# Adaptive normalisation in three instructions per tile, and 56 weight parts moved to VectorE

## The chip, the cores and the metric

The kernel runs on one core of one Trainium2 chip. The metric is the device time of one execution in microseconds (us). The engines are TensorE (PE in the profile; its weight loads are PEld), VectorE (DVE), ScalarE (ACT), GpSimd (POOL) and SyncE (SP), each with a queue of its own that it works through in order.

## The reference

Two layers over 512 latent tokens `x` and 256 context tokens `cx`, 1024 channels, all in float32. What matters here is the modulated norm, which stands twice in each layer, and what is around it:

```python
def rms_norm(t, g):
    return t * rsqrt(mean(t * t, axis=-1) + EPS) * g
def modulate(h, shift, scale):
    return h * (1 + scale) + shift

for l in range(2):
    zx = modulate(rms_norm(x, g_norm1[l]), sh1x, sc1x) @ w_in[l]
    ...                                  # scan branch, gating branch, windowed attention, merged to m
    x = x + ga1x * (m @ w_out[l])
    x = x + ga2x * sq_relu_mlp(modulate(rms_norm(x, g_norm2[l]), sh2x, sc2x), w_ff1[l], w_ff2[l])
    # the same for cx with its own modulation, in layer 0 only (in layer 1 the context gives keys, values, states)
```

## The kernel before, in words

Activations lie transposed: `self.x` is eight tiles of 128 channels by 768 tokens (512 latent, 256 context). Every product of the dense layers is made of three matmuls in the type float32r. Each operand is a rounded high part and a low part (the operand less the high part), and the three are high x high, high x low, low x high. `weights` (line 562) loads a block of 128x1024 weights by a DMA of SP's queue into `wr`, ScalarE rounds it into `wh`, and the low part `wl` is one subtraction, on GpSimd while `self.aside` is set and on VectorE otherwise (line 570). There are three buffers each of `wr`, `wh` and `wl`. The activations that enter a product are split the same way by `split` (line 558), one instruction of ScalarE and one of VectorE.

`norm` (line 826) takes a stretch of tokens. `rms` (line 787) squares the eight tiles on ScalarE and adds them on VectorE, TensorE sums over channels, a chain of 12 tiny VectorE instructions makes the inverse root, and four (or two) more put it on diagonals, which TensorE spreads into PSUM as `p`. Then each of the eight tiles takes four steps: x times `p` on VectorE, scale and bias on ScalarE, rounding on ScalarE, the low part on VectorE.

`out_proj` (line 1350) makes the output projection of the channels `f` from 2 to 7 for one stream of tokens, then the norm of that stream, then the same for the other stream, so that one stream's products can run beside the other's norm. The streams are 512 and 256 tokens wide in layer 0 and 256 and 256 in layer 1. `ff` (line 1378) starts with `ff1(0)`, stream by stream. In layer 0 its tail makes the last `ff2` and the norm of the next layer by streams, then the keys and values (`kv_proj`, `kv_post`) of that layer. `self.aside` is set in the attention stages, in the second part of `out_proj` with `ff1(0)`, and in that tail.

The order of the work is not the program's. `Rec` records every operation, and `schedule` (from line 346 on) plays them through on five modelled engines and writes out an order for each. A candidate with the lower number goes first; weights are recorded as 190 places earlier than they stand, and readers of PSUM as 50 places earlier. `emit` issues that order, so all instructions have line 507. In the model a VectorE operation with two wide inputs in SBUF (`both`) takes longer while GpSimd computes, by the line that the diff changes. The inverse root's chain is a `bundle`, one operation that nothing is put into.

Of the kernel before, what the change touches and what calls it, by code (L numbers as in the profile page):

```python
# [18 lines left out]
F32 = mybir.dt.float32  # L19
# [3 lines left out]
AF = mybir.ActivationFunctionType  # L23
OP = mybir.AluOpType
# [22 lines left out]
PE, ACT, DVE, POOL, SP = range(5)  # L47
# [134 lines left out]
class Rec:  # L182
# [153 lines left out]
    def schedule(self):  # L336
# [31 lines left out]
        free = [0.0] * 5  # L368
# [7 lines left out]
        now = 0.0  # L376
# [3 lines left out]
        def push(t, kind, x):  # L380
            nonlocal seq
            seq += 1
            heapq.heappush(events, (t, seq, kind, x))
# [43 lines left out]
        while events:  # L427
            now = events[0][0]
            while events and events[0][0] <= now + 1e-6:
                _, _, kind, x = heapq.heappop(events)  # L430
                if kind == "rel":
                    used[x.tag] -= 1
                    places[x.tag].append(x)
                    live[x.tag][x.first:x.last + 1] -= 1
                    if x.early:
                        early[x.tag][x.early[0]:x.early[1]] -= 1
            for e in range(5):
                while free[e] <= now + 1e-6:
                    best = pick(e)
                    if best is None:  # L440
                        break
                    _, j, i = best
                    cand[e].pop(j)
                    op = ops[i]
                    for b in op.new:
                        if b.space == "dram":
                            continue
                        used[b.tag] += 1
                        b.early = None
                        b.prev = places[b.tag].pop(0)  # L450
                        if b.prev is None:
                            b.place = fresh[b.tag]
                            fresh[b.tag] += 1
                        else:
                            b.place = b.prev.place
                        if b.first > front:
                            b.early = (front, b.first)
                            early[b.tag][front:b.first] += 1
                    dur = op.dur
                    if op.both and free[POOL] > now and busy:  # L460
                        dur += min(0.7 * (free[POOL] - now), dur)
                    if e == POOL:
                        busy = not op.nbytes
                    if e == ACT and op.table and table not in op.table:
                        dur += 1283
                        table = op.table[0]
                    free[e] = now + dur
                    end = now + dur
                    if op.nbytes:
                        dma = max(dma, end) + op.nbytes / 360.0  # L470
                        end = dma + 1900
                    op.end = end
                    for b in op.psum:
                        b.acc[e] = end
                    order.append((now, i))
                    done[i] = True
                    push(free[e], "go", None)
                    for u in op.users:
                        q = ops[u]
                        r = end + (LAT if op.nbytes else LATS[e][q.eng])  # L480
                        q.ready = max(q.ready, r)
                        q.wait -= 1
                        if q.wait == 0:
                            bisect.insort(cand[q.eng], (q.prio, u))
                            push(q.ready, "go", None)
                    for b in op.bases:
                        b.left -= 1
                        b.end = max(getattr(b, "end", 0.0), end)
                        if b.left == 0 and b.space != "dram":
                            push(b.end + LAT, "rel", b)  # L490
                    while done[front]:
                        front += 1
# [35 lines left out]
class Net:  # L528
# [297 lines left out]
    def norm(self, l, n, hs, G, a, b):  # L826
        nc = self.nc
        (p, _, _), = self.rms([(a, b)])
        i = int(a >= SEQ)
        sh = 24 * n  # L830
        for k in range(KT):
            u = self.slot([128, b - a])
            nc.vector.tensor_mul(u, self.x[k][:, a:b], p)
            nc.scalar.activation(u, u, AF.Identity, scale=G[:, i, k:k + 1], bias=self.mod[l][:, i, sh + k:sh + k + 1])
            self.split(u, hs[k][0][:, a:b], hs[k][1][:, a:b])

    def fm(self, w, hs, W, kk=KT, off=0, stride=128):
        mm = self.nc.tensor.matmul
# [511 lines left out]
    def out_proj(self, l, W):  # L1350
        nc = self.nc
        ms = []
        for k in range(KT):
            h = self.slot([128, W], F32R)
            lo = self.slot([128, W], F32R)
            self.split(self.m[k][:, :W], h, lo)
            ms.append((h, lo))
        self.x = []
        for k in range(KT):
            xk = self.slot([128, W])  # L1360
            nc.sync.dma_start(xk, self.xsrc[k][:, :W])
            self.x.append(xk)
        for i in range(2 if W > SEQ else 1):
            nc.vector.tensor_scalar(self.mod[l][:, i, 16:24], self.mod[l][:, i, 16:24], 0.5, None, op0=OP.mult)
        for f in range(JOINT[0]):
            w = self.weights(l, B_O + f)
            self.residual(l, 16, self.fm(w, ms, W), f)
        hs = self.pairs(W)
        G = self.gain(l, 1, W)
        for z in self.streams(W):  # L1370
            self.aside = True
            for f in range(JOINT[0], KT):
                w = self.weights(l, B_O + f)
                self.residual(l, 16, self.fm(w, ms, [z]), f)
            self.norm(l, 1, hs, G, *z)
        return hs

    def ff(self, l, hs, W):
        nc = self.nc

        def ff1(c, parts):
            out = [(self.slot([128, W], F32R), self.slot([128, W], F32R)) for _ in range(4)]
            for z in parts:
                for j in range(4):
                    w = self.weights(l, B_F1 + 4 * c + j)
                    ps = self.fm(w, hs, z)
                    for p, a, b in ps:
                        r = self.slot([128, b - a])
                        nc.scalar.activation(r, p, AF.Relu)
                        nc.vector.tensor_mul(r, r, r)  # L1390
                        self.split(r, out[j][0][:, a:b], out[j][1][:, a:b])
            return out

        def ff2(c, z, parts):
            for j in range(4):
                w = self.weights(l, B_F2 + 4 * c + j)
                for i in range(2):
                    ps = self.fm(w, z, parts, kk=4, off=i * 128, stride=256)
                    self.residual(l, 40, ps, 2 * j + i)

        z = ff1(0, [[q] for q in self.streams(W)])
        self.aside = False
        for c in range(7):
            for _ in range(3):
                self.bg()
            z2 = ff1(c + 1, [self.parts(W)])
            ff2(c, z, self.parts(W))
            z = z2
        if l == DEPTH - 1:
            ff2(7, z, self.parts(W))  # L1410
            return
        self.aside = True
        self.mod_bias(l + 1, 0, 16)
        hs = self.pairs(TOK)
        G = self.gain(l + 1, 0, TOK)
        ps = [self.p1() for _ in range(6)]
        for q in self.streams(W):
            ff2(7, z, [q])
            self.norm(l + 1, 0, hs, G, *q)
        for toks in (range(4), range(4, 6)):  # L1420
            self.kv_proj(l + 1, hs, ps, toks)
            self.kv_post(l + 1, ps, (0, 1) if toks[0] == 0 else (2,))
        return hs, ps
# [151 lines left out]
```

## Time and profile before

| | |
|---|---|
| median of 3 runs | 2715.12 us (2712.99 to 2715.19) |
| profiled execution, its own time | 2712.24 us |
| its span, first to last instruction | 2710.5 us |
| TensorE busy | 2624.4 us (97%) |
| VectorE busy | 1868.3 us (69%) |
| ScalarE busy | 1239.8 us (46%) |
| GpSimd busy | 319.6 us (12%) |
[...]

The span leaves out 1.7 us of the profiled execution's own time. Busy shares are means over stages. A wait of an engine is shown in square brackets with the instruction that ended it.

### The profile page before, as it was taken

The page shows a single profiled execution, that of the slowest core. Times are in us where ns is not written, and L with a number is a line of the kernel's source. Part 1 is how long each engine was busy: PE and PEld are TensorE (multiplying, and loading weights), DVE is VectorE, ACT ScalarE, POOL GpSimd, SP SyncE. Part 2 cuts the span into 40 slices and gives each one's busy share as a digit, 9 for nine tenths or more (in the row PEclk, how much of TensorE's full clock was granted, in tenths as well). Part 3 has the DMA queues.
Part 4 walks back from the last instruction along what each step waited for, and adds up shares of the span by engine and source line. Part 5 has one row for each costly group of instructions (what it writes and reads, how often), then busy time and mean ns, then how long its engine had stood idle before and what let it go on. Part 6 is the DMA issues. An engine that isn't in the chain of part 4 may idle for free.

```text
span 2710.5 us, 38395 instructions
## 1 busy us (share of the span) xinstructions
PE 2624.4 (97%) x14916; PEld 2259.9 (83%) x14916; DVE 1868.3 (69%) x3528; ACT 1239.8 (46%) x2158; POOL 319.6 (12%) x229
## 2 busy tenths in 40 slices
PE   7999999989999999999999998999999999899999
PEld 4889988878898888888888877887888888888887
DVE  8887787996637758544444478999898666844444
ACT  4466668992122225222222254666996223532322
POOL 1111110111000034000000152120011001600000
PEclk9999999989999999999999989999999999999999
DMA  6112122456524423322222232122347555432322
GB/s 241 59 46 69 67 78 83 124 192 201 167 71 161 166 78 111 115 86 86 86 70 63 70 123 70 59 70 95 94 127 252 200 191 174 138 111 93 94 93 86
DMA packets 94391, 309.15 MB, mean 114 GB/s; under 512 B 11328, under 2 KB 11488, under 8 KB 94208
## 3 DMA queue, kind: packets, MB, share of 16 engines
q1 hardware_dynamic: 74592, 248.62, 28.6%
q0 software_dynamic: 10400, 37.09, 4.6%
q10 hardware_dynamic: 9216, 20.98, 2.0%
q8 instruction: 117, 1.92, 0.3%
q14 instruction: 66, 0.54, 0.1%
HBM read 270.99 MB, written 35.65 MB: 113 GB/s over the span
## 4 chain that ended last, share of the span: by engine, by line
PE 73%; DVE 12%; ACT 6%; DMA 4%; issue 4%; POOL 1%; POOLq 0%; SPq 0%; ACTq 0%; DVEq 0%
PE p L507 73%; DVE s L507 8%; ACT s L507 5%; DVE t L507 3%; DMA wr<-wmod 2%; DMA s<-wmod_k 1%; DVE junk L507 1%; POOL wl L507 1%; ACT wh L507 1%; DMA wr<-w 1%; ACT L507 1%; DVE wl L507 1%; DMA s<-x 0%; DMA gn<-qkg 0%; POOLq L1562 0%
## 5 line engine op out<-in xcount | busy, mean ns | idle before, releaser
L507 PE MATMUL p<-s,wh 128*128 128x512 f32 (+1 forms) x6816 | 1673.9, 353 | 6.3 <-DVE s L507 5.9
L507 PEld LDWEIGHTS p<-s,wh 128*128 128x128 f32 x6816 | 1194.7, 189 | 234.9 <-DVE s L507 7.8
L507 PE MATMUL p<-s,wl 128*128 128x512 f32 (+1 forms) x3408 | 1029.8, 352 | 0.3 <-POOL wl L507 0.3
L507 ACT ACTIVATE wh<-wr 128x1024 fp32r<-128x1024 f32 x340 | 360.4, 1061 | 929.6 <-PE p L507 648.1
L507 PEld LDWEIGHTS p<-s,wl 128*128 128x128 f32 x3408 | 572.2, 189 | 48.0 <-POOL wl L507 0.5
L507 DVE TENSOR_TENSOR wl<-wr,wh 128x1024 fp32r<-128x1024 f32 x240 | 294.7, 1228 | 288.3 <-ACT wh L507 285.8
L507 ACT ACTIVATE s<-p 64x128 f32<-64x128 f32 (+6 forms) x718 | 300.4, 452 | 209.8 <-PE p L507 196.1
L507 POOL TENSOR_TENSOR wl<-wr,wh 128x1024 fp32r<-128x1024 f32 x100 | 244.1, 2444 | 1202.7 <-ACT wh L507 1142.6
L507 DVE TENSOR_TENSOR s<-s,s 128x512 fp32r<-128x512 f32 (+5 forms) x409 | 333.8, 834 | 72.1 <-ACT s L507 68.6
L507 PE MATMUL p<-wh,s 128*128 128x256 f32 (+1 forms) x1472 | 303.7, 301 | 4.1 <-DVE s L507 3.5
L507 PE MATMUL p<-s,s 128*128 128x256 f32 (+3 forms) x1568 | 283.9, 322 | 22.5 <-ACT s L507 16.2
L507 ACT ACTIVATE s<-s 128x256 fp32r<-128x256 f32 (+6 forms) x349 | 203.5, 610 | 213.8 <-DVE s L507 201.2
L507 PEld LDWEIGHTS p<-s,s 128*128 128x128 f32 (+1 forms) x1568 | 222.1, 185 | 60.4 <-ACT s L507 21.1
L507 DVE SCALAR_TENSOR_TENSOR s<-p,mod,s 128x512 f32<-128x512 f32 (+1 forms) x222 | 138.1, 645 | 181.4 <-PE p L507 181.4
L507 PEld LDWEIGHTS p<-wh,s 128*128 128x128 f32 x1472 | 238.9, 191 | 16.8 <-DVE s L507 4.4
L507 DVE TENSOR_TENSOR s<-p,s 64x128 f32<-64x128 f32 (+4 forms) x444 | 201.9, 477 | 29.1 <-ACT s L507 23.1
L507 PE MATMUL p<-wl,s 128*128 128x256 f32 (+1 forms) x736 | 219.6, 298 | 0.4 <-DVE wl L507 0.4
L507 DVE SCALAR_TENSOR_TENSOR junk<-wr,condb 128x1024 bf16<-128x1024 f32 x128 | 156.4, 1222 | 73.1 <-DMA wr<-wmod 71.9
L507 PEld LDWEIGHTS p<-wl,s 128*128 128x128 f32 x736 | 140.2, 190 | 6.3 <-DVE wl L507 0.6
L507 ACT ACTIVATE s<-s,t,t 128x512 f32<-128x512 f32 (+1 forms) x128 | 109.8, 861 | 59.4 <-DVE t L507 59.2
L507 PE MATMUL p<-ident,s 128*128 128x128 f32 (+1 forms) x776 | 106.4, 279 | 23.8 <-DVE s L507 21.7
L507 DVE SCALAR_TENSOR_TENSOR s<-s,s 128x768 f32<-128x768 f32 x128 | 116.2, 950 | 12.5 <-ACT s L507 12.5
(87 smaller groups left out, 1322.7 us busy)
## 6 DMA issues: line engine op xcount, KB each, us to landing
wr<-w SPq DMA_DIRECT2D x340, 512.0 KB, 3.6
wr<-wmod SPq DMA_DIRECT2D x80, 512.0 KB, 4.0
gd<-s ACTq DMA_DIRECT2D x24, 384.0 KB, 2.9
s<-gd POOLq DMA_DIRECT2D x24, 384.0 KB, 5.8
s<-x SPq DMA_DIRECT2D x16, 384.0 KB, 6.4
gd<-s ACTq DMA_DIRECT2D x24, 256.0 KB, 2.1
s<-gd POOLq DMA_DIRECT2D x24, 256.0 KB, 5.6
s<-wmod_k SPq DMA_DIRECT2D x16, 256.0 KB, 6.4
```

The costliest lines, as they stand in the source:

```text
L507: ins = getattr(getattr(self.nc, name), method)(*[r(x) for x in a], **{q: r(x) for q, x in k.items()})
```

## The change

In `norm` the scale moves into VectorE's product with `p`, the shift and the rounding become one ScalarE instruction, and VectorE's second step adds the shift again before it takes off the high part. Two settings of `self.aside` go, so the weights' low parts of `out_proj` from `f` = 2 on, of `ff1(0)`, and of the tail of `ff` are taken on VectorE: 20 blocks in each layer and 16 in the tail, 56 of 100. The other 44, in the attention stages, stay on GpSimd. In `schedule` the modelled delay of a VectorE operation beside GpSimd's becomes all of the time that GpSimd still needs.

```diff
@@ schedule
                     if op.both and free[POOL] > now and busy:
-                        dur += min(0.7 * (free[POOL] - now), dur)
+                        dur += free[POOL] - now
@@ norm
             u = self.slot([128, b - a])
-            nc.vector.tensor_mul(u, self.x[k][:, a:b], p)
-            nc.scalar.activation(u, u, AF.Identity, scale=G[:, i, k:k + 1], bias=self.mod[l][:, i, sh + k:sh + k + 1])
-            self.split(u, hs[k][0][:, a:b], hs[k][1][:, a:b])
+            shift = self.mod[l][:, i, sh + k:sh + k + 1]
+            h, lo = (t[:, a:b] for t in hs[k])
+            nc.vector.scalar_tensor_tensor(u, self.x[k][:, a:b], G[:, i, k:k + 1], p, op0=OP.mult, op1=OP.mult)
+            nc.scalar.activation(h, u, AF.Identity, bias=shift)
+            nc.vector.scalar_tensor_tensor(lo, u, shift, h.bitcast(F32), op0=OP.add, op1=OP.subtract)
@@ out_proj
         for z in self.streams(W):
-            self.aside = True
             for f in range(JOINT[0], KT):
@@ ff, tail
-        self.aside = True
         self.mod_bias(l + 1, 0, 16)
```

## Rows read from the trace of the kernel before

**Rows 1.** Stages: us, busy PE, PEld, DVE, ACT, POOL, granted clock, DMA share, GB/s.

```profile
960.00:1015.00 55.00, 55.00 (x274) 46.09 (x273) 26.25 (x22) 14.90 (x20) 19.89 (x9) 1.00 0.26 78
1015.00:1042.00 27.00, 22.69 (x156) 20.58 (x155) 23.56 (x39) 17.53 (x27) 17.55 (x7) 0.94 0.37 120
...
1530.00:1600.00 70.00, 63.40 (x321) 54.19 (x320) 48.20 (x104) 30.04 (x45) 32.67 (x22) 0.90 0.34 111
1600.00:1640.00 40.00, 33.53 (x149) 27.59 (x148) 32.03 (x75) 19.80 (x38) 19.16 (x8) 0.91 0.37 120
1640.00:1860.00 220.00, 206.37 (x1346) 180.98 (x1344) 197.41 (x559) 138.72 (x318) 41.25 (x17) 0.98 0.19 62
...
2280.00:2370.00 90.00, 81.31 (x561) 76.20 (x560) 67.36 (x108) 46.77 (x85) 48.83 (x20) 0.94 0.40 126
```

**Rows 2.** Timeline of TensorE: start, us, engine, instruction, idle before it and releaser.

```profile
1041.34 0.50 PE L507 MATMUL p<-s,wh 128*128 128x512 f32 x1 [1.80 <-DVE s L507]
...
1575.09 1.87 PE L507 MATMUL p<-ones,s 128*128 128x1 f32 x8 [2.78 <-DVE s L507]
...
1593.20 1.22 PE L507 MATMUL p<-wh,s 128*128 128x512 f32 x2 [3.20 <-DVE s L507]
...
1636.37 0.66 PE L507 MATMUL p<-ident,s 128*128 128x128 f32 x2 [6.47 <-DVE s L507]
...
2345.02 1.01 PE L507 MATMUL p<-ones,s 128*128 128x1 f32 x4 [4.64 <-DVE s L507]
```

**Rows 3.** TensorE alone in stretches of 3 us: busy time, granted clock, DMA.

```profile
1578.00:1581.00 3.00, 3.00 (x16) 0.50 0.58 175
...
1596.00:1599.00 3.00, 3.00 (x9) 0.53 1.03 415
```

**Rows 4.** Timeline, GpSimd (first row) and VectorE, with the count of merged instructions.

```profile
1014.83 2.38 POOL L507 TENSOR_TENSOR wl<-wr,wh 128x1024 fp32r<-128x1024 f32 x1 [3.17 <-ACT wh L507]
...
1015.30 2.45 DVE L507 TENSOR_TENSOR s<-s,s 128x512 f32<-128x512 f32 x1 [0.91 <-ACT s L507]
...
1036.40 4.89 DVE L507 TENSOR_TENSOR s<-s,s 128x512 fp32r<-128x512 f32 x2
...
1548.83 2.03 DVE L507 TENSOR_TENSOR t<-t,t 128x16 f32<-128x16 f32 x1
...
1573.18 1.85 DVE L507 TENSOR_TENSOR s<-s,s 128x512 f32<-128x512 f32 x1 [0.30 <-ACT s L507]
...
1591.24 3.71 DVE L507 TENSOR_TENSOR s<-s,s 128x512 fp32r<-128x512 f32 x4
...
1621.12 1.78 DVE L507 TENSOR_SCALAR t<-t 128x16 f32<-128x16 f32 x4
...
1628.45 2.30 DVE L507 TENSOR_TENSOR t<-t 128x16 f32<-128x16 f32 x1
...
2318.70 1.92 DVE L507 TENSOR_TENSOR s<-s,s 128x256 f32<-128x256 f32 x1 [0.49 <-ACT s L507]
...
2329.99 0.76 DVE L507 TENSOR_TENSOR s<-s,s 128x256 fp32r<-128x256 f32 x2
...
2356.54 5.28 DVE L507 TENSOR_TENSOR s<-s,s 128x256 fp32r<-128x256 f32 x3 [0.20 <-ACT s L507]
```

**Rows 5.** All the instructions of `wl` on GpSimd: ns minimum/median/maximum, first and last start.

```profile
L507 POOL TENSOR_TENSOR wl<-wr,wh x100: 2339/2407/3179, 50.7 to 2366.8; 128x1024 fp32r<-128x1024 f32 x100
```

**Rows 6.** Groups by form, whole span: busy us, mean ns, idle before, releasers.

```profile
L507 DVE TENSOR_TENSOR wl<-wr,wh 128x1024 fp32r<-128x1024 f32 x240 | 294.7, 1228 | 288.3 <-ACT wh L507 285.8
...
L507 DVE SCALAR_TENSOR_TENSOR s<-p,mod,s 128x512 f32<-128x512 f32 x138 | 103.3, 749 | 176.6 <-PE p L507 176.6
...
L507 ACT ACTIVATE s<-s 128x512 fp32r<-128x512 f32 x124 | 76.8, 628 | 95.2 <-DVE s L507 92.2 <-DMA s<-ya 2.0 <-DMA gd<-s 0.5
...
L507 ACT ACTIVATE s<-s,mod,G 128x512 f32<-128x512 f32 x24 | 18.7, 806 | 12.5 <-DVE mod L507 10.1 <-DVE s L507 1.2 <-DVE G L507 1.2
...
L507 DVE TENSOR_TENSOR s<-s,p 128x512 f32<-128x512 f32 x16 | 9.7, 680 | 0.5 <-PE p L507 0.5
```

## The prediction

> **What bounds the kernel now.** I read the stages first, then TensorE's waits in them, then VectorE and GpSimd side by side at the places where TensorE waits. TensorE is busy 97% of the span, so only its gaps, and the time that it runs at a lower clock behind them, can be won. The change touches three regions, and all three have gaps: 960 to 1075 us (second part of the output projection and `ff1(0)`, layer 0), 1530 to 1640 (tail of layer 0, keys and values of layer 1) and 2280 to 2370 (as the first, layer 1). TensorE idles 4.3 us of 1015 to 1042, 6.6 and 6.5 us in the two halves of the second region and 8.7 us in the third [rows 1]. The big waits are all for VectorE: 1.80, 2.78, 3.20, 6.47 and 4.64 us [rows 2].
>
> Behind such a wait the granted clock falls: to 0.50 in 1578 to 1581 and 0.53 in 1596 to 1599, after the waits that ended at 1575.09 and 1593.20 [rows 2, 3]. [...] I read about 6.5 us at that level behind the wait of 2.78 us and 5.5 us behind that of 3.20 us, estimates from such stretches; half of each is lost, 3.2 and 2.8 us. A gap thus costs up to twice what it shows.
>
> Why VectorE is late is seen beside GpSimd. GpSimd's low part runs from 1014.83 to 1017.21. VectorE's addition of 512 columns starts at 1015.30 and ends at 1017.75, 2.45 us, where a product of that size takes 0.68 [rows 4, 6]. It stands still until GpSimd is done. The same happens to instructions of 16 columns, 2.03 us at 1548.83 and 2.30 at 1628.45 [rows 4]. GpSimd is hardly held in return: median 2407 ns, minimum 2339 [rows 5].
>
> **The change part by part.** *Low parts on VectorE.* Removed are 56 GpSimd instructions and every stretch that they cause; added are 56 VectorE instructions of 1.228 us, 68.8 us in all [rows 6]. Where TensorE sets the pace this is hidden: in 960 to 1015 VectorE is busy 26 of 55 us and TensorE all of it [rows 1]. Where VectorE sets the pace, stretch goes out and work comes in, and I set one against the other by place. The stretch of a row is its time less that of unstretched neighbours (0.76 us for two of 256 columns [rows 4], about 0.65 each for 512).
>
> *Norm.* Per 512-column tile ScalarE had 806 + 628 = 1434 ns and will have one instruction with one pointer operand in place of two and a copy. I take the middle, 717 ns; the bounds are 628 and 806 [rows 6]. So a tile's first pair comes some 0.7 us earlier. VectorE's two steps go from about 0.68 each towards 0.749, the three-operand form that reads PSUM and a pointer [rows 6]: +0.13 us a tile, with bounds 0 and +0.2 (the second step doubled), about +1 us for eight tiles of 512 and as much, taken alike, for eight of 256. [...]
>
> *Planner.* The old line granted a blocked operation at most its own duration again: a 16-column one could grow by 0.16 us and grew by 2. The new line costs what the rows show. It can only change orders, now mostly in the attention stages, where 44 of the GpSimd instructions stay. I take 0 there and bounds of 5 us either way, since in layer 1's attention VectorE is busy 197 of 220 us and TensorE idles 13.6 [rows 1].
>
> Now by place.
>
> A, layer 0's output projection. From 1013.6 to 1045.6 VectorE works almost without pause until the first stream's last pair is out, and TensorE waits for pairs. Five stretched rows, the first at 1015.30 and the last at 1036.40 [rows 4], hold 1.8 + 0.6 + 2.1 + 1.3 + 3.6 = 9.3 us. Seven low parts start there: 8.6 us in. The norm adds 1.0. That is -0.3; but VectorE idled 3.7 us there, waiting for ScalarE and TensorE, and the new instructions can fill some 2 of it, and the second stream's norm loses a stretch before a wait of 1.25. Gain 2.5 us, bounds 0 and 7 (all gaps and the slow clock gone).
>
> B1, the wait of 2.78 us at 1575.09. It ends a chain of VectorE and ScalarE that began at 1546. Five stretched rows, 1548.83 to 1573.18 [rows 4], hold 1.85 + 2.15 + 1.2 + 1.2 + 1.15 = 7.6 us. Six low parts come in, 7.4 us, of which 3.4 fit in VectorE's pauses while ScalarE squares. Net 3.6, more than the wait. With 3.2 us of slow clock the place holds 6. Gain 4, bounds 0 and 6.
>
> B2, the wait of 3.20 us at 1593.20 for the first low part. Products of the first eight tiles start at 1586.46; the first subtractions stand in one stretched row of four at 1591.24 [rows 4]. After the change the first tile needs 0.68 + 0.72 + 0.75 and some 0.4 of hand-over: 1589.0. TensorE had its other work until 1588.6. Wait and slow clock hold 6.0 us. Up to three weights' low parts, 3.7 us, may go ahead of that tile. Gain 4, bounds 1 and 6.
>
> B3, the wait of 6.47 us at 1636.37 for the keys. The root's chain held four stretched rows from 1621.12 to 1628.45, 1.1 + 2.15 + 2.15 + 2.1 = 7.5 us. Being a bundle it takes in no low part. But three blocks of the attention stay on GpSimd in 1625 to 1633, and can now meet the rotation that follows: three times about 1.8 us. Gain 4.5, bounds 1 (7.5 less 5.4, less ordering) and 8 (with the clock). [...]
>
> C, layer 1's output projection. From 2318.7 to 2364.5 VectorE sets the pace through both norms. Seven stretched rows, 2318.70 to 2356.54 [rows 4], hold 1.5 + 2.1 + 3.6 + 2.0 + 2.5 + 2.0 + 4.2 = 17.9 us. Ten low parts come in, 12.3 us, and the two norms add 1.9. Net 3.7, and 1.3 of VectorE's pauses filled. Gain 5, bounds 0 and 9.
>
> Sum: 2.5 + 4 + 4 + 4.5 + 5 = 20 us. The profiled execution's own time, 2712.24, would become 2692.2. It lies 2.9 us below the median of the runs, 2715.12, to which the same sum gives 2695.1. I predict 2695.
>
> **The rivals.** *Even exchange.* VectorE gets as much work as stretch goes, and the pauses aren't filled. A gives -0.3, B1 7.6 - 7.4, C 3.7 - 2 for pauses that new waits open; with the low bounds of B2 and B3 that is about 4 us: 2711. For it: in A stretch and work are 9.3 and 9.6. Against it: B3's chain takes in nothing, and B2's tile is shorter whatever the order. Chance 0.18.
>
> *Slower: low parts put ahead of the norm.* Weights have 190 places of priority, so wherever `wh` is out a 1.228 us instruction stands before the norm's steps. In `ff1(0)` of layer 1 four blocks of a stream need 4 x (0.75 + 1.23) us for their squares, splits and low parts beside a norm of 8 x 0.82: 14.5 us of VectorE against about 11.3 of TensorE (four blocks of 24 matmuls at 0.118 us, estimates from the timeline). That opens 3.2 us, and a slow clock behind it 2 more. The like at A, with 4, and two such at B: 2715.1 + 5 + 6 + 5 less B3's 4.5 and what C gains, 5, about 2722. It decides where three or more of VectorE's low parts stand together before a first tile. Against it: TensorE consumes a block in 2.8 us or more, so there is room for only one at a time, and three buffers keep the lead short. Chance 0.10.
>
> *Attention reordered.* The new planner line moves the attention of layer 1, and 5 us are lost or won there. Lost, the time is 2700; won, 2690; both inside the range. Chance that this outweighs the three places: 0.06, half to each side of 0.
>
> The forecast, a gain of 8 to 32 us, keeps 0.66.
>
> **How the numbers follow.** A measurement of this kernel tells about 0.2%, 5.4 us, from no change. Faster by more: 0.66, a third of the even exchange (0.06) and half of the reordering (0.03), 0.75. Same: the rest of the even exchange (0.12) and 0.02: 0.14. Slower: 0.10 and 0.01, 0.11. The range reaches up into the even exchange, 2711. Below, all upper bounds together would give 36 us, 2679; that all come is unlikely, and I set 2681. Outside lie the slower rival and the ends, 0.2.
>
> **What would show it.** Right: 44 low parts on GpSimd and 296 on VectorE; no VectorE instruction of 16 or fewer columns above 1 us in the three regions; one ScalarE instruction a tile, near 0.72 us at 512 columns; waits of TensorE below 1.5 us at B1 and B2; B3 shorter; GpSimd idle in 960 to 1075. The granted clock of 1530 to 1640 should rise from 0.90 to above 0.95. Wrong: low parts of weights on VectorE as the releasers of TensorE's waits, waits in C as long as before with VectorE busy throughout, or new waits in the attention stages. The prediction falls if VectorE's pauses can't take the added work, since the exchange itself is near even.

## The result, and the profile after

The changed kernel takes 2685.91 us (median of four runs, 2684.32 to 2689.07) against 2715.14 before. The ratio is 0.9896, with a 95% interval of 0.9879 to 0.9913. That is 28 us faster by the ratio, where 20 were forecast; the time lies inside the range, near its lower part.

The head of the page after: span, then busy time of each engine.

```profile
span 2683.6 us, 38320 instructions
...
PE 2611.7 (97%) x14916; PEld 2250.1 (84%) x14916; DVE 1860.0 (69%) x3584; ACT 1217.8 (45%) x2108; POOL 182.6 (7%) x173
```

VectorE has 56 instructions more and is busy 8 us less. So 69 us of new work took the place of about as much standing still. By busy time alone the change is an even exchange, and yet the span is 27 us shorter.

The stages after (columns as in [rows 1]), cut where TensorE has done as much work as at the cuts before: a cut lies where it has started matmuls of as many columns, counted from the start, as in the kernel before at 1015, 1042, 1530, 1600, 1640, 1860, 2280 and 2370 us.

```profile
1005.90:1027.50 21.60, 20.78 (x155) 19.15 (x154) 20.70 (x42) 12.45 (x18) 0.00 (x0) 1.00 0.49 148
...
1513.50:1578.20 64.70, 59.09 (x321) 50.27 (x320) 51.26 (x110) 25.69 (x37) 4.34 (x8) 0.97 0.38 123
1578.20:1610.10 31.90, 31.85 (x147) 25.90 (x146) 27.62 (x69) 15.77 (x29) 5.40 (x3) 1.00 0.31 98
1610.10:1834.50 224.40, 208.22 (x1345) 182.31 (x1344) 204.36 (x573) 140.90 (x320) 42.16 (x18) 0.98 0.20 64
1834.50:2259.60 425.10, 417.15 (x2173) 350.51 (x2172) 337.49 (x507) 250.23 (x362) 31.00 (x52) 1.00 0.54 171
2259.60:2343.60 84.00, 78.89 (x561) 74.11 (x560) 62.72 (x130) 40.23 (x68) 0.00 (x0) 0.96 0.48 139
```

The stage from 1860 to 2280 us is not in [rows 1]; before, it was:

```profile
1860.00:2280.00 420.00, 415.30 (x2167) 349.82 (x2168) 335.68 (x504) 252.23 (x364) 30.14 (x52) 1.00 0.54 172
```

TensorE idles 0.8 us in place of 4.3 in the first row, 0.1 for 6.5 in the third and 5.1 for 8.7 in the last, and the granted clock is higher in these three and in the second (over the whole span 0.992 in place of 0.986). The second still idles 5.6 (6.6 before). Two stages became longer: layer 1's attention takes 224.4 us for 220 and idles 16.2 for 13.6, and what lies behind it takes 425.1 for 420.0 and idles 8.0 for 4.7.

TensorE's larger waits after, as in [rows 2]:

```profile
1024.64 0.50 PE L507 MATMUL p<-s,wh 128*128 128x512 f32 x1 [0.65 <-DVE s L507]
...
1572.57 1.22 PE L507 MATMUL p<-wh,s 128*128 128x512 f32 x2 [4.92 <-DVE s L507]
...
1627.00 0.63 PE L507 MATMUL p<-ident,s 128*128 128x128 f32 x4 [1.57 <-DVE s L507]
...
2332.14 0.58 PE L507 MATMUL p<-s,wh 128*128 128x256 f32 x1 [2.21 <-DVE s L507]
```

The waits of 2.78, 6.47 and 4.64 us are gone or small. That of 3.20 us, for the first low part in the tail of layer 0, has grown to 4.92.

The forms that the change made or moved, whole span:

```profile
L507 DVE TENSOR_TENSOR wl<-wr,wh 128x1024 fp32r<-128x1024 f32 x296 | 361.4, 1222 | 316.4 <-ACT wh L507 313.5
...
L507 POOL TENSOR_TENSOR wl<-wr,wh 128x1024 fp32r<-128x1024 f32 x44 | 106.8, 2433 | 534.6 <-ACT wh L507 534.3 <-POOL wl L507 0.4
...
L507 DVE SCALAR_TENSOR_TENSOR s<-s,mod,s 128x512 fp32r<-128x512 f32 x16 | 11.0, 744 | 0.0
L507 DVE SCALAR_TENSOR_TENSOR s<-s,G,p 128x512 f32<-128x512 f32 x16 | 10.9, 741 | 0.0
L507 ACT ACTIVATE s<-s,mod 128x512 fp32r<-128x512 f32 x16 | 10.6, 715 | 3.4 <-DVE s L507 3.4
```

ScalarE's step takes 715 ns where 717 was taken as the middle; VectorE's two take 741 (from PSUM) and 744 (from SBUF), where 749 was the estimate. The two differ by 3 ns.

Where the time came from is read best by stages of equal work, cut in every kernel's trace as above. S0 is layer 0's attention (60 to 400 us in the kernel before), A layer 0's output projection with the start of `ff1(0)` (1015 to 1100), B1, B2 and B3 are the places of the prediction in the tail of layer 0 (1530 to 1575, 1575 to 1600, 1600 to 1640), S1 is layer 1's attention (1640 to 1860), M what lies behind it (1860 to 2280), and C layer 1's output projection (2280 to 2370). The table gives, for one profiled execution of each kernel, the time of a stage against that of the kernel before, in us.

| kernel | S0 | A | B1 | B2 | B3 | S1 | M | C | span |
|---|---|---|---|---|---|---|---|---|---|
| the change | -7.3 | -7.8 | -2.9 | -2.3 | -8.1 | +4.0 | +5.3 | -5.9 | -26.9 |
| planner's line alone | -7.4 | -0.6 | -1.3 | -0.8 | -8.4 | +5.4 | +5.7 | +7.0 | -3.6 |
| norm alone | +0.1 | +0.8 | -1.4 | -3.6 | +4.1 | +1.2 | +4.5 | +1.9 | +4.1 |
| low parts on VectorE alone | +0.1 | -9.0 | -2.9 | -2.3 | -3.6 | +2.0 | +5.3 | -8.1 | -20.3 |
| planner and low parts | -7.3 | -9.0 | -2.9 | -2.2 | -8.1 | +4.5 | +7.2 | -8.0 | -27.1 |
| low parts twice | -7.4 | +2.0 | -3.0 | +4.7 | -8.1 | +9.0 | +6.5 | +10.1 | +9.6 |
| layer 0's attention on VectorE too | -11.4 | -7.7 | -2.9 | -2.2 | -8.1 | +4.6 | +7.2 | -5.3 | -28.0 |
| layer 1's attention on VectorE too | -7.4 | -7.8 | -2.9 | -1.9 | -7.7 | -7.7 | +8.1 | -6.4 | -37.5 |
| all on VectorE | -11.9 | -7.7 | -2.9 | -1.7 | -7.7 | -7.6 | +5.4 | -5.0 | -41.9 |
| pairs first | -7.3 | -8.7 | -3.0 | -8.1 | -7.8 | +9.0 | +8.7 | -8.6 | -30.5 |
| all on VectorE, pairs first | -12.0 | -8.6 | -3.0 | -8.0 | -7.8 | -2.3 | +5.5 | -8.4 | -44.7 |
| the same, norm in four steps | -12.1 | -9.2 | -3.0 | -4.4 | -8.4 | -3.0 | +7.8 | -8.4 | -41.4 |

The orders differ between kernels, so a stage is the same amount of TensorE's work and only nearly the same matmuls. The stretches left out are edited by no run (the first norm of layer 0 has code of its own and keeps its four steps). One of them, 1100 to 1530 us, agrees within 0.6 us in all kernels; the others, ahead of 60 and from 400 to 1015 us, differ by up to some 3 from kernel to kernel. A single difference below 3 us is therefore not read here.

### The profile page after: what moved, and what is told of

The parts are those of the page before. It is cut to its first block, busy times and chain, and to the rows that moved or that the text cites. A ratio compares the mean times of both kernels' runs of the same rounds, so it can differ in the third digit from the quotient of the medians.

```text
span 2683.6 us, 38320 instructions
## 1 busy us (share of the span) xinstructions
PE 2611.7 (97%) x14916; PEld 2250.1 (84%) x14916; DVE 1860.0 (69%) x3584; ACT 1217.8 (45%) x2108; POOL 182.6 (7%) x173
## 4 chain that ended last, share of the span: by engine, by line
PE 79%; DVE 10%; ACT 6%; issue 2%; DMA 2%; SPq 0%; POOL 0%; ACTq 0%; DVEq 0%; POOLq 0%
PE p L507 79%; DVE s L507 7%; ACT s L507 5%; DVE t L507 2%; DVE wl L507 1%; DMA s<-wmod 1%; ACT wh L507 1%; ACT L507 1%; DVE junk L507 1%; DMA wr<-wmod 0%; DMA wr<-w 0%; DMA s<-wmod_k 0%; DMA s<-gd 0%; SPq L507 0%; POOL s L507 0%
## 5 line engine op out<-in xcount | busy, mean ns | idle before, releaser
L507 DVE TENSOR_TENSOR wl<-wr,wh 128x1024 fp32r<-128x1024 f32 x296 | 361.4, 1222 | 316.4 <-ACT wh L507 313.5
L507 PE MATMUL p<-s,s 128*128 128x256 f32 (+3 forms) x1568 | 286.9, 324 | 17.9 <-ACT s L507 13.6
L507 DVE TENSOR_TENSOR s<-s,s 128x512 fp32r<-128x512 f32 (+5 forms) x361 | 260.3, 735 | 53.8 <-ACT s L507 51.2
L507 ACT ACTIVATE s<-s 128x512 fp32r<-128x512 f32 (+6 forms) x301 | 183.7, 631 | 189.0 <-DVE s L507 175.9
L507 PEld LDWEIGHTS p<-s,s 128*128 128x128 f32 (+1 forms) x1568 | 221.6, 185 | 50.0 <-ACT s L507 17.9
L507 POOL TENSOR_TENSOR wl<-wr,wh 128x1024 fp32r<-128x1024 f32 x44 | 106.8, 2433 | 534.6 <-ACT wh L507 534.3
L507 PE MATMUL p<-ident,s 128*128 128x128 f32 (+1 forms) x776 | 112.3, 280 | 18.4 <-DVE s L507 16.0
```

The source lines that it names most:

```text
L507: ins = getattr(getattr(self.nc, name), method)(*[r(x) for x in a], **{q: r(x) for q, x in k.items()})
```

## The experiments

**One part at a time.** Four kernels take the change apart. The planner's line alone:

```diff
-                        dur += min(0.7 * (free[POOL] - now), dur)
+                        dur += free[POOL] - now
```

> The planner's line alone; norm in four steps and all 100 low parts on GpSimd as before. Theory 1 (the places): the gain of the change in 960 to 1085, 1530 to 1640 and 2280 to 2370 us comes from taking GpSimd's low parts out. Then this run keeps only what was gained ahead of the first output projection (about 9 us there), gives some of it back in layer 1's attention, and ends at 2704 to 2713. Theory 2 (the planner): the orders were wrong because the model did not know the delay, and knowing it is most of the gain. Then TensorE's waits in the three regions shrink with GpSimd still at work in them, and the time is 2690 to 2698.

Measured: 2707.0 us, ratio 0.9974 (0.9964 to 0.9983), 7 us faster. Theory 1 holds. The gain, 7.4 us, lies in layer 0's attention, before any instruction that the rest of the change edits; as much is lost again in layer 1's output projection, where GpSimd is still at work. At B3 8.4 us are won, and the two stages behind it lose 11. TensorE's waits of this kernel in 2260 to 2375 us (total, times, longest):

```profile
PE p L507 <- DVE s L507: 9.5, 5, 4.3
```

One sign of theory 2 came true all the same. TensorE's wait for the keys, 6.47 us before, is 0.76 here, although VectorE still stands still beside GpSimd in the root's chain ahead of it (2.33 us for 16 columns, 0.18 in the changed kernel):

```profile
1609.89 2.33 DVE L507 TENSOR_TENSOR t<-t 128x16 f32<-128x16 f32 x1
...
1623.37 0.44 PE L507 MATMUL p<-ident,s 128*128 128x128 f32 x2 [0.76 <-DVE s L507]
```

With the new line the planner puts matmuls of 256 columns ahead of this one that stood behind it before.

The norm alone, with its three instructions as in the diff of the change:

```diff
-            nc.vector.tensor_mul(u, self.x[k][:, a:b], p)
-            nc.scalar.activation(u, u, AF.Identity, scale=..., bias=...)
-            self.split(u, ...)
+            nc.vector.scalar_tensor_tensor(u, self.x[k][:, a:b], G[:, i, k:k + 1], p, op0=OP.mult, op1=OP.mult)
+            nc.scalar.activation(h, u, AF.Identity, bias=shift)
+            nc.vector.scalar_tensor_tensor(lo, u, shift, h.bitcast(F32), op0=OP.add, op1=OP.subtract)
```

> The norm in three steps alone, planner and low parts as before. Theory 1: a first pair comes some 0.7 us earlier per norm and VectorE's steps are 0.13 us longer; 2710 to 2716. Theory 3 (ScalarE): the chain of the norm hangs on ScalarE's two steps, and the shorter chain is worth 8 us or more: below 2707.

Measured: 2715.15 us, ratio 1.0008 (0.9999 to 1.0018). The norm in three steps is worth nothing by itself, as theory 1 had it. Theory 3 falls.

The low parts on VectorE alone:

```diff
         for z in self.streams(W):
-            self.aside = True
...
-        self.aside = True
         self.mod_bias(l + 1, 0, 16)
```

> The 56 low parts on VectorE alone, norm in four steps and the old planner line. Theory 1: 2695 to 2703, no stretched VectorE row left in the three regions, and nothing changed ahead of 960 us. Theory 2: VectorE takes as much work as stretch goes, and the time is within 6 us of before.

Measured: 2690.91 us, ratio 0.9916 (0.9901 to 0.9931), 23 us faster, which is more than theory 1 had allowed. This is the change's core, and most of it lies in the two output projections (A and C in the table). Theory 2 falls for the low parts. At the keys a wait of 3.78 us is left, so there the low parts take away less than half of the 6.47 us:

```profile
1619.65 0.56 PE L507 MATMUL p<-ident,s 128*128 128x128 f32 x2 [3.78 <-DVE s L507]
```

The planner's line and the low parts, with the norm in four steps:

> Planner's line and low parts on VectorE, norm in four steps. Theory 1: the norm's part is 3 us or less, so 2686 to 2691. Theory 3: at least 8 us slower than the whole change, 2694 or more.

Measured: 2685.89 us, ratio 0.9899 (0.9884 to 0.9914): the whole change, within the intervals, so the norm adds nothing here either. 23, 7 and -2 us by the parts add up to the 28 of the whole.

**The same work twice.** If new work on VectorE costs little because it falls into pauses, more of it should cost little too. `twice` is set where the change took `aside` away.

```diff
         (self.nc.gpsimd if self.aside else self.nc.vector).tensor_sub(lo, raw, hi.bitcast(F32))
+        if self.twice:
+            self.nc.vector.tensor_sub(lo, raw, hi.bitcast(F32))
```

> The changed kernel, but each of the 56 low parts on VectorE is written twice, so 68 us more of VectorE's work in the three regions, known to the planner. Theory 1a (what counts is where the work lies): a low part on VectorE falls into its pauses or behind work that TensorE does not wait for, and costs little; the second ones cost 10 us or less, 2686 to 2696. Theory 1b (the prediction's bookkeeping): a low part takes its 1.23 us from VectorE's chain wherever VectorE sets the pace, 8.6 us in A, 4 in B and 12.3 in C; the second ones cost 20 to 30 us, 2706 to 2716.

Measured: 2724.47 us, ratio 1.0047 (1.0032 to 1.0062), some 40 us more than the changed kernel for 68 us of work. Theory 1a falls, and 1b was still too cheap. Against the change the doubled parts cost 10 us in A, 7 at B2, 16 in C and 5 in layer 1's attention, which this run does not edit; at B1 and B3 they cost nothing. Its waits of TensorE for VectorE, in 960 to 1100 and in 2240 to 2400 us:

```profile
PE p L507 <- DVE s L507: 8.1, 2, 7.8
...
PE p L507 <- DVE s L507: 14.9, 5, 5.0
```

So in A, at B2 and in C VectorE's work lies on the path. That the first set of low parts nevertheless came with a gain of 23 us means that the stretch which it replaced, with the GpSimd work that made it, had cost more than the low parts do. Each of the two prices by itself was not measured.

**The attention stages.** The same exchange was made where the change leaves it out, first in layer 0 alone (the diff below) and in layer 1 alone (with `l == 0` in its place):

```diff
-            self.aside = True
+            self.aside = l > 0
             self.attention(l, hs, W, ps)
```

> The changed kernel with the 24 low parts of layer 0's attention on VectorE too. About 23 us of stretch goes from 62 to 400 us and 29 us of work comes. Theory 1a: the work can be put aside and the stretch could not, so TensorE's waits there (5 us for VectorE) shrink: 2680 to 2685. Theory 1b: an exchange that costs 6 us of VectorE, of which TensorE's pace hides most: 2685 to 2690.

Measured: 2684.71 us, ratio 0.9900 (0.9885 to 0.9915): nothing beside the change's 0.9896, and no decision between the two theories. In its trace the stage itself is 4.1 us shorter than the change's (S0 in the table), and the rest of the kernel loses about as much.

> The changed kernel with the 20 low parts of layer 1's attention on VectorE too. About 32 us of stretch goes from 1600 to 1860 us and 24 us of work comes, in a stage where VectorE is busy nine tenths of the time. Theory 1a: 2674 to 2682. Theory 1b: the net of 8 us is seen at most in part: 2680 to 2684. A rival (VectorE becomes the bound): its queue is full there, and the time is 2686 or more.

Measured: 2675.78 us, ratio 0.9868 (0.9851 to 0.9884), 8 us faster than the change. The rival, that VectorE becomes the bound, falls.

Both, with `self.aside = False`, so that GpSimd computes no low part at all:

> All 100 low parts on VectorE. The sum of the two runs with one attention each: theory 1a 2668 to 2680; the rival that VectorE becomes the bound: 2686 or more. No VectorE instruction is stretched after 62 us.

Measured: 2670.41 us, ratio 0.9846 (0.9832 to 0.9861), inside theory 1a. Layer 1's attention in this kernel, cut at the same work (columns as in [rows 1]):

```profile
1605.90:1818.70 212.80, 205.94 (x1345) 180.52 (x1344) 198.75 (x592) 139.69 (x316) 0.00 (x0) 0.99 0.20 66
```

TensorE idles 6.9 us in place of 16.2 in the changed kernel's row. VectorE's busy time there fell by 5.6 us (198.75 against 204.36), although 20 low parts, 24 us of work, were added: they took the place of standing still, which counts as busy. With no low part left on GpSimd, no VectorE instruction of 16 or fewer columns takes 0.9 us or more; before, 17 did, and in the changed kernel five, all in the attention stages. So it was GpSimd's low parts that stretched them.

**Pairs first.** The wait of 4.92 us wanted a cause. ScalarE had the first tile rounded at 1566.9 us. VectorE's timeline of the changed kernel behind it:

```profile
1565.37 2.71 DVE L507 SCALAR_TENSOR_TENSOR s<-s,G,p 128x512 f32<-128x512 f32 x4
1568.00 1.22 DVE L507 TENSOR_TENSOR wl<-wr,wh 128x1024 fp32r<-128x1024 f32 x1
1569.13 2.71 DVE L507 SCALAR_TENSOR_TENSOR s<-s,G,p 128x512 f32<-128x512 f32 x4
1571.77 4.72 DVE L507 SCALAR_TENSOR_TENSOR s<-s,mod,s 128x512 fp32r<-128x512 f32 x7
```

All eight products and a low part of weights stand ahead of the first tile's low part. The products read `p` in PSUM, and the planner puts readers of PSUM 50 places ahead. The experiment takes that away from the norm's product alone:

```diff
+            self.rec.boost, was = -DRAINS, self.rec.boost
             nc.vector.scalar_tensor_tensor(u, self.x[k][:, a:b], G[:, i, k:k + 1], p, op0=OP.mult, op1=OP.mult)
+            self.rec.boost = was
```

> The changed kernel, but the norm's product with p loses the 50 places that readers of PSUM are put ahead, so a tile's low part can be taken before the later tiles' products. Theory 4 (the planner's priority holds back the first pair): TensorE's wait of 4.92 us for the first pair in the tail of layer 0 falls below 1.5, the smaller ones in the two output projections (0.65 and 2.21 us) shrink too, and the time is 2677 to 2682. Rival (VectorE's throughput): the last pair is what counts, the wait moves to later tiles and the time stays within 2 us of the changed kernel, 2684 to 2688.

Measured: 2682.83 us, ratio 0.9891 (0.9875 to 0.9908). The cause is shown: VectorE takes the first low part after three products, and TensorE's wait is 0.49 us.

```profile
1560.95 2.06 DVE L507 SCALAR_TENSOR_TENSOR s<-s,G,p 128x512 f32<-128x512 f32 x3
1562.92 0.75 DVE L507 SCALAR_TENSOR_TENSOR s<-s,mod,s 128x512 fp32r<-128x512 f32 x1
...
1563.72 0.73 PE L507 MATMUL p<-wh,s 128*128 128x512 f32 x2 [0.49 <-DVE s L507]
```

In time it is 3 us, less than the two intervals can tell apart, and it falls between the two forecasts. By the table B2 is 5.8 us shorter than with the change, and layer 1's attention behind it 5.0 us longer (229.4 us, of which VectorE is busy 206.6). That VectorE's amount of work then sets the time of that stage is likely by this row, but no run shows it.

The same with all low parts on VectorE, with three steps and with four:

> As the run before, with all 100 low parts on VectorE. If both effects add: 2662 to 2667, against 2670 of the kernel with all low parts on VectorE. If VectorE's throughput decides: 2668 to 2672.

Measured: 2667.78 us, ratio 0.9833 (0.9818 to 0.9848), the fastest of all; it lies 2.6 us below the kernel without this edit, again inside the intervals and between the forecasts. B2 is 6.3 us shorter, layer 1's attention 5.3 longer.

> As the run before, but with the norm in four steps, as before the change. Theory 4: with pairs in order of tiles the 0.7 us of ScalarE per tile lies ahead of the first pair and of each that follows, and ScalarE (1.43 us a tile) is as slow as VectorE; 2 to 6 us slower than the run with three steps. Rival: the norm's steps are worth nothing in either order, within 2 us.

Measured: 2670.55 us, ratio 0.9843 (0.9828 to 0.9857), 2.8 us slower than with three steps. The sign is that of theory 4, the size is not resolved. In the trace it lies at B2, which is 3.6 us longer.

## Why the prediction was right, and where its terms were off

**What bounds the kernel.** Right. In the three regions most gaps came from VectorE standing still beside GpSimd. With GpSimd's low parts out of them TensorE's gaps shrink (stages above), and the low parts alone give 23 of 28 us. The stretches go where GpSimd's low parts go: of VectorE's instructions of 16 or fewer columns, 17 took 0.9 us or more before, five after, and none with all low parts on VectorE. Which instructions stand still was read from rows alone; no run changed that. In the kernel before, of those that began behind the start of a low part on GpSimd, with 0.5 us or more of it still to run, the eight products `s<-s,p` of 512 columns, which read PSUM, took 0.68 to 0.69 us, and the five that met no low part 0.68. Ten additions `s<-s,s` of that size took 1.85 to 2.49, where the median of those that met none is 0.69, and four TENSOR_SCALAR `s<-s,t`, with one tile and a column, 2.57 to 2.59 for 0.48.

**The sum: right in part by luck.** The five places of the prediction gave 27 us where 20 were forecast. Layer 0's attention gave 7 that I had not booked, and layer 1's attention and what lies behind it, taken at 0 as well, took 9 back. That the stages taken at 0 nearly cancel is luck.

**The planner's line, taken at 0: mis-sized.** Alone it is worth 7 us. The six kernels that have it, with layer 0's attention otherwise as before, are 7.3 or 7.4 us shorter there, and the two without it 0.1 longer. Before and after:

```profile
60.10:400.10 340.00, 330.77 (x2221) 297.57 (x2221) 276.25 (x778) 204.61 (x488) 55.30 (x23) 0.99 0.19 60
```

```profile
59.40:392.10 332.70, 327.65 (x2222) 295.90 (x2221) 272.54 (x779) 204.32 (x487) 55.20 (x23) 1.00 0.19 61
```

The bound of 5 was too narrow. I had looked for the effect in layer 1's attention, where VectorE is fullest; it came in layer 0's.

**A, taken at 2.5: too small, 7.8**, above its upper bound. (The five stretched rows add up to 9.4 us, not 9.3.) The low parts alone give 9.0 there, the planner's line 0.6. The second stream's part, 1042 to 1100 us, has 2.3 of the 7.8.

**B1, taken at 4: 2.9**, and the wait is gone; the slow clock behind it lies in B2's stretch. The rows showed another cause that I had not booked. GpSimd's queue also issues the loads of the constants. Before, they stood behind low parts that waited for ScalarE; now they don't. From GpSimd's timeline, before (with VectorE's wait) and then after:

```profile
1531.66 2.39 POOL L507 TENSOR_TENSOR wl<-wr,wh 128x1024 fp32r<-128x1024 f32 x1 [457.87 <-ACT wh L507]
1533.99 0.56 POOL L507 DMA_DIRECT2D s<-rope  x1
...
1542.36 0.56 POOL L507 DMA_DIRECT2D gn<-qkg  x1
...
1546.20 0.43 DVE L507 TENSOR_TENSOR tab<-s,gn 128x256 f32<-128x256 f32 x1 [2.07 <-DMA gn<-qkg]
```

```profile
1476.66 0.54 POOL L507 DMA_DIRECT2D s<-rope  x1 [586.59 <-issue]
1477.19 0.54 POOL L507 DMA_DIRECT2D gn<-qkg  x1
```

VectorE's wait for `gn` is gone with that. Whether it is part of B1's gain is not shown: the load of `gn` is issued at 1491 us with the norm alone and at 1532 with the planner's line alone, and the wait that B1 is about is the same in both, 1.38 and 1.40 us.

**B2, taken at 4: wrong in its mechanism.** "After the change the first tile needs 0.68 + 0.72 + 0.75 and some 0.4 of hand-over" left out that seven other products go ahead by the planner's rule. The kernel before had them in that order already, ahead of the row at 1591.24 that the prediction quotes:

```profile
1586.46 4.86 DVE L507 TENSOR_TENSOR s<-s,p 128x512 f32<-128x512 f32 x8
```

The wait grew from 3.20 to 4.92 us, where the prediction wanted it below 1.5. The place is 2.3 us shorter all the same, since TensorE's granted clock rose in it, from 0.73 to 0.92 (before and after):

```profile
1575.00:1600.00 25.00, 21.08 (x102) 18.56 (x103) 19.39 (x48) 15.24 (x26) 13.87 (x12) 0.73 0.50 167
```

```profile
1555.60:1578.20 22.60, 17.00 (x105) 14.55 (x104) 21.85 (x48) 12.15 (x20) 0.00 (x0) 0.92 0.37 120
```

Part of that is the slow clock behind B1's wait, 3.2 us, which was booked with B1. Here the shorter chain per tile did not help TensorE's wait, with eight tiles' first steps in front in the queue. With pairs first the wait is 0.49 us, and B2 gives 8.1.

**B3, taken at 4.5: the wait went, but mostly for another reason.** The root's chain is 16-column instructions of 0.17 to 0.18 us again, as foreseen, and the largest wait until 1660 us is 1.57. But with the planner's line alone the wait goes too, with the chain as stretched as before, and with the low parts alone 3.78 us of it stay. So the new order by itself takes the wait away, and the shorter chain by itself is worth 3.6 of the 8.1 us. As the lower bound had it, GpSimd's three remaining blocks, at 1603.99, 1606.83 and 1609.62 us, stretch the rotation behind it (4.12 us for two products that take 0.68 each where they meet no low part):

```profile
1605.44 4.12 DVE L507 TENSOR_TENSOR s<-s,tab 128x512 f32<-128x512 f32 x2
```

Of the 8.1 us layer 1's attention gives 4.0 back; with the planner's line alone it gives back 5.4 of 8.4. What lies behind the attention (M) is 4.5 to 8.7 us longer in all kernels than before, with the norm alone too, and no run edits it on purpose. That stays open.

**C, taken at 5: right, 5.9.** Ten low parts for 17.9 us of stretch was the sum, and it held, although TensorE still waits 2.21 and 1.70 us there.

**The rivals.** The even exchange is what the busy times show (VectorE 1868 before, 1860 after) and is not what the time shows. The slower rival named a real danger: in the 4.92 us one low part ahead of a first tile is 1.22 (the products are the most of it). With twice the work it comes true. The attention was reordered, as the third rival had it, in both layers.

## What to carry to other kernels

VectorE's standing still beside GpSimd was counted as busy here (the addition of 2.45 us [rows 4], 0.69 where it meets no low part); look for instructions of one form with two durations, and ask what the other engine does in the long ones. Work that is taken over can cost its time on the path, as the doubled run shows (some 40 us for 68 us of work), so exchange it only against stretch that lies on the path as well. Where a planner fixes the orders, a shorter chain is worth what its priorities leave of it: read the order in which the first of several tiles comes out before booking a gain for it.

## What the runs showed that was not expected

The stretch at the lower granted clock behind a gap was not longer for a longer gap. Before, a wait of 3.20 us was followed by an estimated 5.5 us at that level (0.53 in 1596 to 1599 us [rows 3]). After, a wait of 4.92 us, in TensorE's stretches of 3 us:

```profile
1569.00:1572.00 3.00, 0.00 (x0) 1.00 0.45 154
1572.00:1575.00 3.00, 2.44 (x6) 0.52 0.05 20
1575.00:1578.00 3.00, 3.00 (x14) 0.91 0.02 5
```

The first row is idle throughout, at a granted clock of 1.00. The lower level, taken as 0.50 [rows 3], makes up an estimated 3.4 us of the two others (they lack 0.48 and 0.09 of the full clock over 3 us, and the lower level lacks a half), for a longer gap than before; 0.4 of it lies in the gap itself. So the gap cost about 1.5 us more than it shows, half of the 3 us behind it, where the prediction had allowed for up to as much again. Three other kernels wait the same 4.92 us at this place (all on VectorE, and the two with one attention each), and behind the wait I read 3 to 4 us at the lower level in them, estimates from granted clocks of 0.50 and then 0.85 (all), 0.50 and 0.93 (layer 0's), 0.76 and 0.56 (layer 1's) in 1565 to 1570 and 1570 to 1575 us. No run changed the length of a gap alone.
